# Routing per token tile, the norm vector folded into the router weights, and one expert of three groups moved to the conditional second round

## The chip, the cores and the metric

The kernel runs on one core of a Trainium2 chip. The metric is the time of one execution on the device, in microseconds (us), the median of three runs. TensorE (PE, with its weight loads listed as PEld), VectorE (DVE), ScalarE (ACT), GpSimd (POOL) and SyncE (SP) each work through a queue of their own; SP issues nearly all the weight loads. Lines (L107) are those of the kernel before, unless said otherwise.

## What is computed

Two transformer blocks on 256 tokens of width 1024, all in float32. The change is in the last part, a mixture of experts with two levels of routing. Cut to what matters:

```python
t = rmsnorm(h, norm_ffn)                                  # 256 x 1024
group_logits = t @ w_router_group                         # 8 groups
g_sel = argmax(group_logits);  p_group = softmax(group_logits)[g_sel]
in_group = (t @ w_router_expert).reshape(n, 8, 8)[rows, g_sel]
top_logit, top_local = top_k(in_group, 2)                 # 2 of the group's 8 experts
gate = softmax(top_logit) * p_group
hid = silu(x_e @ w_gate[e]) * (x_e @ w_up[e])             # 1024 -> 512, for each of 64 experts
y  += gate * (hid @ w_down[e])                            # 512 -> 1024
out = rmsnorm(h + y, norm_final)
```

The weights of one expert are three matrices of 2 MB each, so the 64 experts hold 403 MB, and most of the kernel's time goes into them.

## The kernel before

**Weights.** A float32 matrix is multiplied as two halves in a rounded type: `split` (L103 to L112) makes the high half `whi` on ACT (the hi cast) and the rest `wlo` on DVE (the lo, which reads whi), 128x1024 elements each, in buffers six deep. Each matmul of the program is then two or three on PE.

**Before the experts.** `out_proj` adds the output projection into the residual `xres`, for each of two token tiles t (128 tokens) and two column halves n. The four last pairs of weight rows are held back, so that the results come at the end one after another, (t, n) = (0,0), (0,1), (1,0), (1,1), and `router` is called for each. When both halves of a tile are there, it multiplies by the norm's gain `g_f2` into `tA`, transposes tA, multiplies by the router weights `wr` into the logits `lg` and scales by 1/rms. After both tiles a second piece of code picks each token's group (`G`, with `first_max`), its rank among the tokens of that group (`prk`, a matmul with a triangle of ones) and `key0`, the slot of tokens of group 0.

**The visits.** `moe` goes through groups of tokens in "visits": group 0, experts 0 to 2, first, because its weights can be loaded before the routing is known; then seven groups in order of size (place 1 is the smallest; which group that is, is known on the chip alone, in `which`), and group 0's experts 3 to 7 last. Place 7, the largest, has 128 slots and three products for each matmul ("large"); the others have 64 slots, where both halves of the tokens lie side by side and two products do. `prepare` makes the one-hot matrix `oh` of a visit, gathers its tokens by matmuls with tA (`pgx`), copies them (`xghi`, hi on ACT and lo on DVE) and gathers the gates of the visit's experts (`pgw`, from `wsel`). For each expert follow gate and up (`pgu`, 32 matmuls in a small visit), the activation, and down (`pd`). `plan` sorts the groups and makes their keys; `weights` makes wsel; `count` counts the tokens of each expert (`manyx`).

**Loads.** Weights go through a ring of 11 buffers of 1 MB, six loads for an expert (the last expert's down matrix in four halves of a load instead of two). SP issues them in order, each as soon as its buffer has been read. From the fourth expert on a load carries a condition: an expert with no tokens isn't loaded, but its buffers are passed over and all its arithmetic is done on what lies in them. The fourth expert's loads need `which` and `manyx`.

**The second round.** Tokens that find no slot in their group are counted by `beyond`; if there are any (`flag`), a second call of `moe` under a runtime condition takes two groups with 128 slots each, 16 experts.

**Order.** The order of instructions on each engine is set when the program is built, by a scheduler that goes by a cost model and by priorities (`with soon()` gives a high one), and by `fence`, which puts one instruction behind another. In the first visit the list `after` holds the fences of six splits: the first two have none, the next four stand behind the last copy of the router (`last_tT`). From step 8 of moe on (the end of the first expert's gate and up) PE, ACT and DVE keep the order of the program.

```python
on = after.pop() if after else None
for x in both:
    fence(x, on)
```

Of the kernel before, what the change touches and what calls it, by code (L numbers as in the profile page):

```python
# [32 lines left out]
def mega(ctx, tc, a, out, dbg=None):  # L33
# [978 lines left out]
    tAT = {}  # L1012

    rsq, last_tT = {}, [None]

    def router(t, n, ps):
        add_res(t, n, ps)
        if n == 0:
            rsq[t] = gp.tile([P, D], F32, tag="xn", name="xn"), sm.tile([P, 2], F32, tag="sh", name="sh")
        xn, ss = rsq[t]  # L1020
        nc.scalar.activation(xn[:, cols(n)], xres[:, t, cols(n)], AF.Square, accum_out=ss[:, n:n + 1])
        if n == 0:
            return
        if t == 0:
            tAT["A"] = mp.tile([P, NT, KD, P], F32, name="tA")
        tA = tAT["A"]
        tT = [mq.tile([P, 4, P], F32, tag="hid", name="tT") for _ in range(2)]
        by_k = lambda x: x.rearrange("q (p k) -> q k p", k=KD)
        for q in range(2):
            ks = slice(4 * q, 4 * q + 4)  # L1030
            nc.vector.tensor_tensor(tA[:, t, ks], by_k(xres[:, t, :])[:, ks], by_k(g_f2)[:, ks], op=OP.mult)
            ps = mm.tile([P, 4, P], F32, tag="mm", name="tps")
            for i in range(4):
                nc.tensor.transpose(ps[:, i, :], tA[:, t, 4 * q + i, :], ident)
            last_tT[0] = nc.scalar.copy(tT[q], ps)
        rs = inv_root(mean_sq(ss))
        ps = mm.tile([P, 512], F32, tag="mm", name="plg")
        for k in range(KD):
            nc.tensor.matmul(ps[:, :72], tT[k // 4][:, k % 4, :], wr[:, k, :], start=k == 0, stop=k == KD - 1)
        nc.vector.tensor_scalar(lg[:, t, :], ps[:, :72], rs, None, op0=OP.mult)  # L1040
        nc.vector.tensor_scalar(tA[:, t], tA[:, t], rs, None, op0=OP.mult)
# [3 lines left out]
    tA = tAT["A"]  # L1045
    dump("h1", xres)

    with soon():
        rdx = cst.tile([P, 8], F32, name="rdx")
        nc.gpsimd.iota(rdx, pattern=[[-1, 8]], base=8, channel_multiplier=0, allow_small_or_imprecise_dtypes=True)  # L1050
        slot = mp.tile([P, P], F32, name="slot")
        nc.gpsimd.iota(slot, pattern=[[1, P]], base=0, channel_multiplier=0, allow_small_or_imprecise_dtypes=True)
        slot2 = mp.tile([P, P], F32, name="slot2")
        nc.gpsimd.iota(slot2, pattern=[[0, 2], [1, GS]], base=0, channel_multiplier=0, allow_small_or_imprecise_dtypes=True)
        r1 = lambda n: mp.tile([P, NT], F32, name=n)
        r8 = lambda n: mp.tile([P, NT, 8], F32, name=n)

        def first_max(x, mx, oh):
            nt = x.shape[1]
            b8 = lambda x: x[:, :, None].to_broadcast([P, nt, 8])  # L1060
            nc.vector.tensor_reduce(mx, x, AX.X, OP.max)
            nc.vector.tensor_tensor(oh, x, b8(mx), op=OP.is_equal)
            nc.vector.tensor_tensor(oh, oh, rdx[:, None, :].to_broadcast([P, nt, 8]), op=OP.mult)
            m2 = sm.tile([P, nt], F32, tag="fm", name="fm")
            nc.vector.tensor_reduce(m2, oh, AX.X, OP.max)
# [510 lines left out]
```

## Time and profile before

| what | value |
|---|---|
| median of 3 runs | 1646.37 us (1645.75 to 1648.77) |
| profiled execution | 1646.35 us, its span 1644.6 us |
| PE busy | 1606.0 us, 98% of the span |
| DVE busy | 1353.3 us, 82% |
| ACT busy | 1148.5 us, 70% |
| DMA | 493.55 MB, 300 GB/s in the mean |

A matmul's end is modelled in such a profile, so that PE at 98% means that there is nearly always a matmul under way, not that the engine is at its peak. The shares are means over stages with different limits: the experts take the last 990 us, and it is there that the change is read.

### The profile page before, as it was taken

Reading aid. Unit: us, or ns where it says so; the run is one execution under the profiler, and the core shown is the slowest. Engines: PE = TensorE matmul, PEld = TensorE weight load, DVE = VectorE, ACT = ScalarE, POOL = GpSimd, SP = SyncE. Lnnn points to the kernel's source line nnn. Section 1 sums busy time; section 2 is a strip of 40 time slices with the busy share of each in tenths; the row PEclk is TensorE's granted clock in tenths of the full one; section 3 lists DMA queues with packets and bytes.
Section 4 is the critical chain, followed back from the end, with each engine's and each line's share of the span. In section 5 each row is a group of like instructions: output and inputs, shape, how many; then the busy total and the mean of one; then the engine's idle time right before and its main releaser. Section 6 shows DMA issues by size and latency. Waiting matters only on the chain. (4 is left out here: it accounts for less than half of the span.)

```text
span 1644.6 us, 24374 instructions
## 1 busy us (share of the span) xinstructions
PE 1606.0 (98%) x8474; PEld 1302.4 (79%) x8474; DVE 1353.3 (82%) x1643; ACT 1148.5 (70%) x1544; POOL 44.7 (3%) x69
## 2 busy tenths in 40 slices
PE   8999999999999998999999999999999999999996
PEld 7898788998798877777767777778877777777774
DVE  6666675555868886799999999998999899999997
ACT  5355554444556643788878888877788888888886
POOL 1000010000100130000000000000000000000000
PEclk9999999999999998999999999999999999999999
DMA  9953455555663337797997999999999999999991
GB/s 323 273 175 130 142 171 201 180 189 170 173 182 122 116 132 298 271 421 325 385 392 315 380 421 421 421 412 363 347 380 420 409 421 420 421 420 420 421 375 48
DMA packets 124884, 493.55 MB, mean 300 GB/s; under 512 B 9149, under 2 KB 53537, under 8 KB 78160
## 3 DMA queue, kind: packets, MB, share of 16 engines
q1 hardware_dynamic: 120160, 484.47, 76.9%
q0 software_dynamic: 1952, 6.05, 1.3%
q10 hardware_dynamic: 2640, 1.38, 0.3%
q8 instruction: 69, 1.13, 0.3%
q14 instruction: 63, 0.52, 0.1%
HBM read 509.30 MB, written 1.44 MB: 311 GB/s over the span
## 5 line engine op out<-in xcount | busy, mean ns | idle before, releaser
L107 DVE TENSOR_TENSOR wlo<-ring,whi 128x1024 fp32r<-128x1024 f32 x714 | 839.9, 1219 | 63.4 <-ACT whi L107 59.8
L107 ACT CAST whi<-ring 128x1024 fp32r<-128x1024 f32 x714 | 712.3, 1048 | 74.0 <-PE pgu L1279 20.9
L1279 PE MATMUL pgu<-whi,xghi 128*128 128x512 f32 x896 | 356.6, 398 | 1.4 <-DVE xghi L1216 1.4
L1280 PE MATMUL pgu<-wlo,xghi 128*128 128x512 f32 x896 | 352.8, 394 | 1.1 <-DVE wlo L107 1.1
L107 DVE TENSOR_TENSOR wlo<-raw,whi 128x1024 fp32r<-128x1024 f32 x173 | 211.8, 1232 | 135.6 <-ACT whi L107 134.3
L107 ACT CAST whi<-raw 128x1024 fp32r<-128x1024 f32 x173 | 180.3, 1048 | 188.9 <-PE pb L115 81.0
L1280 PEld LDWEIGHTS pgu<-wlo,xghi 128*128 128x128 f32 x896 | 169.4, 189 | 37.4 <-DVE wlo L107 3.4
L1279 PEld LDWEIGHTS pgu<-whi,xghi 128*128 128x128 f32 x896 | 169.4, 189 | 35.3 <-DVE xghi L1216 1.6
L114 PE MATMUL pb<-hThi,whi 128*128 128x256 f32 x480 | 137.5, 286 | 0.2 <-ACT hThi L129 0.2
L1279 PE MATMUL pd<-whi,hidThi 128*128 128x512 f32 x332 | 136.5, 411 | 0.9 <-DVE hidThi L1299 0.8
L115 PE MATMUL pb<-hTlo,whi 128*128 128x256 f32 x480 | 135.8, 283 | 0.5 <-DVE hTlo L130 0.5
L116 PE MATMUL pb<-hThi,wlo 128*128 128x256 f32 x480 | 135.7, 283 | 0.0
L1280 PE MATMUL pd<-wlo,hidThi 128*128 128x512 f32 x332 | 130.9, 394 | 0.0
L1289 PEld LDWEIGHTS pht<-pairs,gu 128*128 128x128 f32 x896 | 108.6, 191 | 4.9
L1289 PE MATMUL pht<-pairs,gu 128*128 128x64 f32 x896 | 106.0, 271 | 0.0
L1389 PE MATMUL pd<-ring,hs 128*64 128x512 f32 x216 | 104.2, 605 | 0.0
L1279 PEld LDWEIGHTS pd<-whi,hidThi 128*128 128x128 f32 x332 | 62.2, 187 | 52.8 <-ACT whi L107 36.1
L115 PEld LDWEIGHTS pb<-hTlo,whi 128*128 128x128 f32 x480 | 91.9, 191 | 1.4 <-DVE hTlo L130 0.7
L114 PEld LDWEIGHTS pb<-hThi,whi 128*128 128x128 f32 x480 | 91.9, 191 | 1.2 <-ACT hThi L129 0.5
L116 PEld LDWEIGHTS pb<-hThi,wlo 128*128 128x128 f32 x480 | 91.8, 191 | 0.0
L114 PE MATMUL pa<-whi,hThi 128*128 128x512 f32 x216 | 87.0, 406 | 3.3 <-ACT whi L107 1.7
L116 PE MATMUL pa<-whi,hTlo 128*128 128x512 f32 x216 | 85.6, 399 | 1.2 <-DVE hTlo L130 1.2
(432 smaller groups left out, 2260.1 us busy)
## 6 DMA issues: line engine op xcount, KB each, us to landing
ring<-in_w_gate_dram SPq DMA_DIRECT2D x128, 1024.0 KB, 9.9
ring<-in_w_up_dram SPq DMA_DIRECT2D x128, 1024.0 KB, 10.6
ring<-in_w_down_dram SPq DMA_DIRECT2D x126, 1024.0 KB, 9.2
raw<-in_w_in_dram SPq DMA_DIRECT2D x38, 1024.0 KB, 5.4
raw<-in_w_ff_dram SPq DMA_DIRECT2D x32, 1024.0 KB, 5.0
raw<-in_w_out_dram SPq DMA_DIRECT2D x12, 1024.0 KB, 5.0
raw<-in_w_in_dram SPq DMA_DIRECT2D x9, 512.0 KB, 4.8
raw<-in_w_ple_gate_dram SPq DMA_DIRECT2D x4, 1024.0 KB, 5.0
```

What stands on the lines that cost most here:

```text
L107: both = [nc.scalar.copy(hi, raw), nc.vector.tensor_tensor(lo, raw, hi.bitcast(F32), op=OP.subtract)]
L114: nc.tensor.matmul(ps, l[0][lsel], r[0][rsel], start=first, stop=False)
L115: nc.tensor.matmul(ps, l[0][lsel], r[1][rsel], start=False, stop=False)
L116: nc.tensor.matmul(ps, l[1][lsel], r[0][rsel], start=False, stop=last)
L1279: nc.tensor.matmul(ps, x[0][:, k, :], w[0][wsel], start=first, stop=False)
L1280: nc.tensor.matmul(ps, x[0][:, k, :], w[1][wsel], start=False, stop=last)
L1289: nc.tensor.matmul(ps[:, j, q, :], x[:, ts(q)], pairs, start=True, stop=True)
L1389: nc.tensor.matmul(pds[v][m][:GS, :], h[:, 3, :], wt[:, 0, cols(m)], start=False, stop=False)
```

## The change

Five parts. (1) The router's input is transposed straight from xres, each half as it is ready; the gain goes into the router weights once (`wr` times `gcol`, a new load of the gain by column), and three weight tensors get another order in memory on the host, so that rows fit. (2) Group, rank, key, one-hot and the gather of group 0 are done in `router`, for each token tile. (3) In `split` only the lo is fenced, and the fences of moe stand behind the last one-hot (`last_oh`). (4) `weights`, `plan` and `count` are called after steps 0, 3 and 4 of moe instead of ahead of it (the first two) and after step 0. (5) For group 0 (among experts 3 to 7) and places 1 and 2, `count` finds the expert with the fewest tokens, `trade` swaps it with expert 7 in the lists of names, counts and gates, and the last name of each list is left out of the visits. If any of the three has a token (`left`), the flag is set, and the second round then does these three as well as its 16.

```diff
-        for x in both:
-            fence(x, on)
+        fence(both[1], on)
...
+    gcol = mp.tile([P, KD], F32, name="gcol")
+    nc.gpsimd.dma_start(gcol, a["norm_ffn_2"].rearrange("(k p) -> p k", p=P))
+    nc.vector.tensor_tensor(wr, wr, gcol[:, :, None].to_broadcast([P, KD, NG + NG * NE]), op=OP.mult)
...
     def router(t, n, ps):
         add_res(t, n, ps)
...
+        tps = mm.tile([P, 4, P], F32, tag="mm", name="tps")
+        for i in range(4):
+            nc.tensor.transpose(tps[:, i, :], xres[:, t, (4 * n + i) * P:(4 * n + i + 1) * P], ident)
         nc.scalar.activation(xn[:, cols(n)], xres[:, t, cols(n)], AF.Square, accum_out=ss[:, n:n + 1])
+        tT = mq.tile([P, 4, P], F32, tag="hid", name="tT")
+        nc.scalar.copy(tT, tps)
+        for i in range(4):
+            nc.tensor.matmul(plg[t][:, :72], tT[:, i, :], wr[:, 4 * n + i, :], start=n + i == 0, stop=n + i == 4)
         if n == 0:
             return
+        rs = inv_root(mean_sq(ss))
+        nc.vector.tensor_scalar(lg[:, t, :], plg[t][:, :72], rs, None, op0=OP.mult)
+        tt_ = slice(t, t + 1)
+        first_max(lg[:, tt_, :8], gm[:, tt_], G[:, tt_])
+        ps = mm.tile([P, 512], F32, tag="mm", name="prk")
+        nc.tensor.matmul(ps[:, :8], ltm, G[:, t, :], start=True, stop=t == 0)
+        if t:
+            nc.tensor.matmul(ps[:, :8], ones, G[:, 0, :], start=False, stop=True)
+        nc.vector.scalar_tensor_tensor(tA[:, t].rearrange("p k f -> p (k f)"), xres[:, t, :], rs, g_f2, op0=OP.mult, op1=OP.mult)
...
+        last_oh[0] = nc.vector.tensor_scalar(oh0[:, t, :], slot2, key0[:, tt_], None, op0=OP.is_equal)
         if t == 0:
+            pgx0.append(acc.tile([P, KD, GS], F32, tag="acc", name="pgx"))
         for k in range(KD):
+            nc.tensor.matmul(pgx0[0][:, k, :], tA[:, t, k, :], oh0[:, t, :GS], start=t + k == 0, stop=t + k == KD)
...
-                nc.vector.tensor_scalar(ovi[:, 0:1], m, 0.0, None, op0=OP.is_gt)
+                nc.vector.tensor_tensor(ovi[:, 0:1], m, left, op=OP.max)
+                nc.vector.tensor_scalar(ovi[:, 0:1], ovi[:, 0:1], 0.0, None, op0=OP.is_gt)
...
+    def trade(x, at, n):
+        d, both = mp.tile([P, n, 8], F32, name="trd"), mp.tile([P, n], F32, name="trs")
+        nc.vector.tensor_tensor(d, x[:, :, 7:8].to_broadcast([P, n, 8]), x, op=OP.subtract)
+        nc.vector.tensor_tensor(d, d, at, op=OP.mult)
+        nc.vector.tensor_reduce(both, d, AX.X, OP.add)
+        nc.vector.tensor_tensor(x, x, d, op=OP.add)
+        nc.vector.tensor_tensor(x[:, :, 7], x[:, :, 7], both, op=OP.subtract)
...
+        nc.vector.scalar_tensor_tensor(few, many[:, :NS], 16.0, by3(rdx), op0=OP.mult, op1=OP.add)
+        nc.vector.memset(few[:, 0, :3], 1e6)
+        nc.vector.tensor_reduce(fewest, few, AX.X, OP.min)
+        nc.vector.tensor_tensor(few, few, fewest[:, :, None].to_broadcast([P, NS, 8]), op=OP.is_equal)
...
+        trade(many[:, :NS], few, NS)
+        trade(names, few, NS)
...
+        nc.vector.tensor_copy(namesx, names)
+        nc.vector.tensor_reduce(left, many[:, :NS, NE - 1], AX.X, OP.max)
...
+        nc.vector.tensor_copy(wsel2, wsel)
+        trade(wsel2, mine, NT)
...
-            for f in begin[:2]:
-                f()
-        after[:] = [last_tT[0]] * 4 + [None] * 2 if skip else []
+        after[:] = [last_oh[0]] * 4 + [None] * 2 if skip else []
...
                 if s == 0:
                     with soon():
+                        for f in begin[:1]:
+                            f()
                         finish([[0, prep]])
-                        for f in begin[2:]:
-                            f()
+                if 3 <= s < 2 + len(begin):
+                    begin[s - 2]()
...
     def in_order(g, e):
-        if g == 0:
-            return e
+        if g < NS:
+            return bass.ds(value(namesx[0:1, g, e:e + 1], NG * NE - 1), 1) if g or e > 2 else e
...
-        [(0, every[:3])] + [(g, every[3 * (g == 0):]) for g in (1, 2, 3, 7, 4, 5, 6, 0)],
-        small=lambda g: g < NG - 1, skip=True, begin=(plan, weights, count), on_the_way=beyond())
+        [(0, every[:3])] + [(g, every[3 * (g == 0):NE - (g < NS)]) for g in (1, 2, 3, 7, 4, 5, 6, 0)],
+        small=lambda g: g < NG - 1, skip=True, begin=(weights, plan, count), on_the_way=beyond())
...
     with tc.If(flag > 0):
+        for x in range(NS):
+            moe(lambda g: [(keys[:, t, g:g + 1] if g else key0[:, t:t + 1]) for t in range(NT)],
+                lambda g, e: bass.ds(lasts[g], 1), [(x, [NE - 1])], small=lambda g: True)
```

What the scheduler makes of it shows at three places. The first is the end of the output projection. On ACT, `xn,sh` are the squares of a half of xres (x3 and the last are those of all four halves), `tT` the copies of the transposed halves, and the `whi` are hi casts of the first experts' weights. Before:

```order
L1021 ACTIVATE xn,sh<-xres 128x512 x3
L1035 COPY tT<-tps 128x512
L1021 ACTIVATE xn,sh<-xres 128x512
L1035 COPY tT<-tps 128x512 x3
L107 CAST whi<-ring 128x1024 x4
```

and now:

```order
L1051 ACTIVATE xn,sh<-xres 128x512 x2
L1053 COPY tT<-tps 128x512
L107 CAST whi<-ring 128x1024
L1051 ACTIVATE xn,sh<-xres 128x512
L107 CAST whi<-ring 128x1024 x3
L1051 ACTIVATE xn,sh<-xres 128x512
L1053 COPY tT<-tps 128x512 x3
L1095 ACTIVATE tmp<-tmp 128x16
```

The four casts have moved from behind the router's copies to ahead of the last two squares. On DVE the same place now reads as follows (`xres<-xres,po` are the last two additions to the residual, `ms` the mean squares, `lg` the first tile's logits):

```order
L290 TENSOR_TENSOR xres<-xres,po 128x512
L272 TENSOR_SCALAR ms<-sh 128x1
L290 TENSOR_TENSOR xres<-xres,po 128x512
L273 SCALAR_TENSOR_TENSOR ms<-sh,ms 128x1
L1016 TENSOR_TENSOR wr<-wr,gcol 128x576
L1067 SCALAR_TENSOR_TENSOR tA<-xres,rs,g_f_5759 128x1024
L1059 TENSOR_SCALAR lg<-plg,rs 128x72
```

The product of wr and gcol, which every logit needs, stands behind the mean square of the second tile.

The second place is PE behind the output projection's last matmul (`po`): `plg` are the logits, `prk` the ranks, `pgx` the gather of group 0, `poh` a transpose of its one-hot. Before:

```order
L116 MATMUL po<-whi,hTlo 128x512
L1034 MATMUL tps<-ident,tA 128x128 x8
L1039 MATMUL plg<-wr,tT 128x72 x4
L1034 MATMUL tps<-ident,tA 128x128 x8
L1039 MATMUL plg<-wr,tT 128x72 x12
L1075 MATMUL prk<-G,ltm 128x8 x2
L1077 MATMUL prk<-G,ones 128x8
```

and now:

```order
L115 MATMUL po<-whi,hTlo 128x512
L1055 MATMUL plg<-wr,tT 128x72
L1050 MATMUL tps<-ident,xres 128x128 x4
L1055 MATMUL plg<-wr,tT 128x72 x7
L1064 MATMUL prk<-G,ltm 128x8
L1050 MATMUL tps<-ident,xres 128x128 x4
L1076 MATMUL pgx<-oh,tA 128x64 x3
L1290 MATMUL poh<-ident,oh 128x128
L1076 MATMUL pgx<-oh,tA 128x64 x5
L1055 MATMUL plg<-wr,tT 128x72
L1050 MATMUL tps<-ident,xres 128x128 x4
L1055 MATMUL plg<-wr,tT 128x72 x7
```

The logits of both tiles stood together, ahead of both ranks; now the rank and the gather of the first tile stand between them.

The third place is PE ahead of the second expert's gate, the `pgu` behind `pgw`; `pct<-sel` are the counts of each expert's tokens, `pgx` the gather of the next visit, and `wsel_6049` is the new wsel2. Before, the counts stood at the first expert's first matmul, and the second expert's gate began so:

```order
L1233 MATMUL pgx<-oh,tA 128x64 x13
L1245 MATMUL pgw<-wsel,oh 128x8 x2
L1248 MATMUL poh<-ident,oh 128x128 x2
L1279 MATMUL pgu<-whi,xghi 128x512
L1280 MATMUL pgu<-wlo,xghi 128x512
```

and now:

```order
L1322 MATMUL pgu<-wlo,xghi 128x512
L1217 MATMUL pct<-sel,ones 128x64 x2
L1276 MATMUL pgx<-oh,tA 128x64 x8
L1290 MATMUL poh<-ident,oh 128x128
L1276 MATMUL pgx<-oh,tA 128x64 x8
L1290 MATMUL poh<-ident,oh 128x128
L1287 MATMUL pgw<-wsel_6049,oh 128x8 x2
L1321 MATMUL pgu<-whi,xghi 128x512
```

The counts, the whole gather and the gates from wsel2, the last product of `count`, now stand between the first expert's up and the second expert's gate.

## Rows read from the trace of the kernel before

**Rows 1.** Windows: PE, PEld, DVE, ACT, POOL busy (instructions), granted clock, DMA share, GB/s.

```profile
1300.00:1400.00 100.00, 100.00 (x480) 76.03 (x479) 94.46 (x99) 85.19 (x107) 0.00 (x0) 1.00 1.01 421
```

**Rows 2.** Waits from 700 to 1600 us: in total, times, longest.

```profile
ACT whi L107 <- DMA ring<-in_w_down_dram: 0.7, 2, 0.3
```

**Rows 3.** SP's timeline in place 2: the down loads of three experts in turn.

```profile
911.28 0.66 SPq L99 DMA_DIRECT2D ring<-in_w_down_dram  x2
...
925.22 1.16 SPq L99 DMA_DIRECT2D ring<-in_w_down_dram  x2
...
939.15 1.14 SPq L99 DMA_DIRECT2D ring<-in_w_down_dram  x2
```

**Rows 4.** DMA moved and issued from 652 to 1638 us, with median us to landing.

```profile
q1 hardware_dynamic: 50976, 369.12, 92.4%
...
ring<-in_w_down_dram SPq DMA_DIRECT2D x124, 1024.0 KB, 9.2
ring<-in_w_gate_dram SPq DMA_DIRECT2D x122, 1024.0 KB, 9.4
ring<-in_w_up_dram SPq DMA_DIRECT2D x122, 1024.0 KB, 10.7
```

**Rows 5.** The view of rows 1 in two stretches of 14 us.

```profile
766.00:780.00 14.00, 14.00 (x84) 11.34 (x84) 11.23 (x14) 10.22 (x14) 0.00 (x0) 1.00 0.38 138
884.00:898.00 14.00, 14.00 (x76) 11.06 (x75) 13.14 (x15) 10.83 (x14) 0.00 (x0) 1.00 0.34 132
```

**Rows 6.** The DMA view of rows 4, from 1545 to 1570 us.

```profile
ring<-in_w_down_dram SPq DMA_DIRECT2D x4, 1024.0 KB, 17.4
```

**Rows 7.** PE's timeline: start, duration, and idle time ahead with its releaser.

```profile
633.84 0.39 PE L116 MATMUL po<-whi,hTlo 128*128 128x512 f32 x1
...
646.54 0.57 PE L1075 MATMUL prk<-G,ltm 128*128 128x8 f32 x2 [5.64 <-DVE G L1066]
...
652.00 3.51 PE L1233 MATMUL pgx<-oh,tA 128*128 128x64 f32 x16
656.92 0.80 PE L1279 MATMUL pgu<-whi,xghi 128*128 128x512 f32 x1 [1.40 <-DVE xghi L1216]
...
672.71 0.48 PE L1279 MATMUL pgu<-whi,xghi 128*128 128x512 f32 x1
```

**Rows 8.** ACT's timeline: the square of the last half of xres.

```profile
635.24 0.63 ACT L1021 ACTIVATE xn<-xres 128x512 f32<-128x512 f32 x1
```

**Rows 9.** The page's groups of instructions: the two halves of a split, mean ns.

```profile
L107 DVE TENSOR_TENSOR wlo<-ring,whi 128x1024 fp32r<-128x1024 f32 x714 | 839.9, 1219 | 63.4 <-ACT whi L107 59.8
L107 ACT CAST whi<-ring 128x1024 fp32r<-128x1024 f32 x714 | 712.3, 1048 | 74.0 <-PE pgu L1279 20.9
```

**Rows 10.** DVE's timeline in the routing and the plan.

```profile
639.18 0.28 DVE L1040 TENSOR_SCALAR lg<-plg,rs 128x72 f32<-128x72 f32 x1
...
640.29 0.17 DVE L1066 TENSOR_TENSOR G<-G,fm 128x8 f32<-128x8 f32 x1
...
646.23 0.17 DVE L1066 TENSOR_TENSOR G<-G,fm 128x8 f32<-128x8 f32 x1
...
648.21 0.28 DVE L1225 TENSOR_SCALAR oh<-slot,key 128x128 f32<-128x128 f32 x1
...
651.94 0.17 DVE L1129 SCALAR_TENSOR_TENSOR size<-pct,rdx 128x8 f32<-128x8 f32 x1 [1.23 <-PE pct L1123]
...
655.41 0.18 DVE L1152 TENSOR_TENSOR keys<-keys,rank 128x16 f32<-128x16 f32 x1
...
658.41 0.17 DVE L1251 COPY gw<-pgw 128x8 f32<-128x8 f32 x1 [1.54 <-PE pgw L1245]
658.49 0.47 DVE L1225 TENSOR_SCALAR oh<-slot,keys 128x128 f32<-128x128 f32 x2
```

**Rows 11.** The view of rows 1 during the first expert's gate.

```profile
657.00:664.00 7.00, 7.00 (x21) 5.84 (x22) 2.91 (x6) 2.32 (x3) 0.00 (x0) 0.50 0.01 2
```

**Rows 12.** DMA issues from 560 to 650 us: the router weights' smaller load.

```profile
wr<-in_w_router_group_dram POOLq DMA_DIRECT2D x1, 32.0 KB, 6.6
```

More of the change, by code (lines that the diff above doesn't have):

```diff
@@ L1043, in mega @@
     for _ in wo2:
         pass
-    tA = tAT["A"]
     dump("h1", xres)
[L1048 to L1065, printed above, removed]
-            nc.vector.tensor_tensor(oh, oh, b8(m2), op=OP.is_equal)
-        gm, G, tmp, rank, key0 = r1("gm"), r8("G"), r8("tmp"), r1("rank"), r1("key0")
-        ranked = []
-        for t in range(NT):
-            tt_ = slice(t, t + 1)
-            first_max(lg[:, tt_, :8], gm[:, tt_], G[:, tt_])
-            ps = mm.tile([P, 512], F32, tag="mm", name="prk")
-            nc.tensor.matmul(ps[:, :8], ltm, G[:, t, :], start=True, stop=t == 0)
-            if t:
-                ranked.append(nc.tensor.matmul(ps[:, :8], ones, G[:, 0, :], start=False, stop=True))
-            nc.vector.tensor_scalar(key0[:, tt_], G[:, t, 0:1], -4096.0, 4096.0, op0=OP.mult, op1=OP.add)
-            nc.vector.tensor_tensor(tmp[:, t, :], ps[:, :8], G[:, t, :], op=OP.mult)
-            nc.vector.tensor_reduce(rank[:, tt_], tmp[:, t, :], AX.X, OP.add)
-            nc.vector.tensor_tensor(key0[:, tt_], key0[:, tt_], rank[:, tt_], op=OP.add)
@@ L1118, in weights @@
         dump("wsel", wsel)
+    at_ = mp.tile([P, 8], F32, name="at_")
     def plan():
@@ L1192, in beyond @@
         beyonds["flag"] = nc.values_load(ovx[0:1, 0:1], min_val=0, max_val=1, skip_runtime_bounds_check_because="it is 0 or 1")
+    NS = 3
+    namesx = mp.tile([P, NS, 8], I32, name="namesx")
+    left = mp.tile([P, 1], F32, name="left")
+    wsel2 = r8("wsel2")
+    def trade(x, at, n):
[5 more added lines that the diff above has]
+        nc.vector.tensor_tensor(x[:, :, 7], x[:, :, 7], both, op=OP.subtract)
     def count():
@@ L1219, in two, with prepare @@
         return x.rearrange("p k (a b) -> p k a b", a=2)
-    def prepare(keys, b, small, xgs, gws, v):
-        oh = mq.tile([P, NT, P], F32, name="oh", bufs=1)
-        for t in range(NT):
-            nc.vector.tensor_scalar(oh[:, t, :], slot2 if small else slot, keys[t], None, op0=OP.is_equal)
-        yield
+    def prepare(keys, b, small, xgs, gws, v, wsel):
         xg = [x[:, b] for x in xgb]
@@ L1229, in prepare @@
         kn = 512 // w
-        pss = [acc.tile([P, kn, w], F32, tag="acc", name="pgx") for _ in range(KD // kn)]
-        for t in range(NT):
+        oh, pss = oh0, pgx0[:]
+        if not pss:
+            oh = mq.tile([P, NT, P], F32, name="oh", bufs=1)
+            for t in range(NT):
+                nc.vector.tensor_scalar(oh[:, t, :], slot2 if small else slot, keys[t], None, op0=OP.is_equal)
+            yield
+            pss = [acc.tile([P, kn, w], F32, tag="acc", name="pgx") for _ in range(KD // kn)]
+        for t in range(0 if pgx0 else NT):
             for k in range(KD):
-                x = nc.tensor.matmul(pss[k // kn][:, k % kn, :], tA[:, t, k, :], oh[:, t, :w],
+                nc.tensor.matmul(pss[k // kn][:, k % kn, :], tA[:, t, k, :], oh[:, t, :w],
                                      start=t == 0 and k % kn == 0, stop=t == 1 and k % kn == kn - 1)
-                if t + k == 0 and ranked:
-                    fence(x, ranked.pop())
         yield AHEAD
@@ L1240, in prepare @@
             halves(two(xg[0]), ps) if small else split_ps(xg[0][:, ks, :], xg[1][:, ks, :], ps)
+        pgx0.clear()
         xgs[v] = xg
@@ L1337, in mega, with moe @@
     AHEAD = 3
-    def moe(keys, expert, visits, small=lambda g: False, skip=False, begin=(), on_the_way=iter(())):
+    weights_ = wsel
+    def moe(keys, expert, visits, small=lambda g: False, skip=False, begin=(), on_the_way=iter(()), wsel=wsel2):
+        first = weights_ if skip else wsel
         todo = [(v, g, e, es) for v, (g, es) in enumerate(visits) for e in es]
@@ L1426, in follow @@
                     g2 = visits[v + 1][0]
-                    steps.append([1, prepare(keys(g2), (v + 1) % 2, small(g2), xgs, gws, v + 1)])
+                    steps.append([1, prepare(keys(g2), (v + 1) % 2, small(g2), xgs, gws, v + 1, wsel)])
                 if i == 0 and kind == "u" and last:
```

72 lines of the change are left out of this document (47 added, 25 removed).

## Prediction

> **What bounds the kernel now.** I read the windows by stage first. In a stretch of small visits PE is busy all the time, DVE 94%, and DMA runs at 421 GB/s [rows 1]: three limits close together, so the question is which ends last. The waits decide it: over nearly the whole expert stage ACT waits 0.7 us in all for a down load to land [rows 2], so the loads come in time and the chain of hi cast, lo and matmul sets the pace. That pace is the distance from one expert's loads to the next on SP, which follows the reading of the buffers: 13.94 and 13.93 us [rows 3]. DMA is right behind: six loads of 1.049 MB at 421 GB/s are 14.94 us, more than 13.93, and only the extra work where a visit ends lets the loads keep up.
>
> **Do the three experts fall away at all?** The change rests on three experts without a token, one in each of group 0's late list and places 1 and 2; otherwise the flag is set. From 652 to 1638 us SP issued 124, 122 and 122 loads of 1.0486 MB, and the last expert's four halves, 387.97 MB, but 369.12 MB moved [rows 4]. The 18.85 MB that are missing are 18 loads, which is three experts. Two holes in the DMA stand at 766 and 884 us, 138 and 132 GB/s [rows 5]; a third must be hidden in the backlog near the end. They are 118 us apart, eight experts of 13.93 and 6.6 for what a visit adds, so they have the same place in two visits that follow each other. The reference's inputs, worked through in float32, give the same: expert 6 of groups 0, 6 and 5 has no token, and those are group 0 and the two smallest. No group overflows. So the lists lose just these three and the flag stays 0.
>
> **Term 1, three experts less.** Their loads were skipped already; what goes is their arithmetic, which has no condition. A buffer's turn is 11 loads of 13.93/6 us, 25.5 us, so the expert that left the hole at 884 us is worked off from about 910 us; there SP's rows keep the same pace [rows 3], and an empty expert costs as much as another. 3 x 13.93 = 41.8 us. The cover for this saving is the ring: without the holes the loads must keep up for 25 experts from the start to the large visit. From 1545 to 1570 us, after 24 small experts since the large one, a load lands 17.4 us after its issue [rows 6], of the 25.5 of a turn. So 24 experts used up all but 8 us, and 25 should just pass; the large visit then refills the lead. I take 41.8 and keep a loss of up to 8 us for a rival.
>
> **Term 2, the first expert's start.** Before, the last matmul of the output projection starts at 633.84 and the first expert's at 656.92 [rows 7], 23.1 us later. The order now, from that last matmul (L, 0.5 us later than before because four transposes stand in front of it):
> The unfenced hi casts stand ahead of the last square on ACT. Each needs a buffer that the held-back rows release only with their last matmuls, and takes 1.05 us [rows 9]; three in a row from there put the square at about L+3.3, where it was 1.4 behind [rows 8, 7].
> Behind it DVE has the mean square, the wr product (an estimate of 0.7 from the lo's 1.22 by elements [rows 9]) and only then PE the first tile's logits: 24 short instructions of 0.11 us. (The gather's sixteen took 3.51 us at half clock, 0.22 each [rows 7]; I use 0.11 at full clock.) Logits at L+8.
> The first tile's choice of group took 1.28 us (639.18 to 640.46 [rows 10]); with rank, key and one-hot 2.8: L+10.8.
> PE then has the first gather ahead of the second tile's logits: 18 instructions, four transposes, a copy of 0.6, the last logits: 4.2 us at full clock, 7.5 at half. Second logits at L+15 to 18.3.
> Its choice is again 1.28, and from G to the end of the one-hot 2.1 (646.40 to 648.49 [rows 10]): L+18.4 to 21.7.
> DVE then has four fenced lo's, 4.9 us, and four small operations ahead of the lo of the gathered tokens, 0.7, while gather and copy take 2.6 to 4.5: first expert at L+24.7 to 28.0, against 23.1. With L's 0.5 that is +2.1 to +5.4; if the casts don't hold the square, +0.2. I take +4. So the earlier selection buys nothing here: what was parallel over two tiles is now one tile after the other, and the scheduler has put the whole of it behind the output projection.
> The new load gcol is in pieces of 4 bytes, as many as the 32 KB router load has, which landed in 6.6 us [rows 12]; it is issued right behind the router loads, which were there for the first logits before, and its product stands late by its place on DVE, so it costs nothing. If it comes later than that product's turn, term 2 grows by the rest.
>
> **Term 3, the second expert's start.** Before, the second expert's gate began at 672.71, 15.8 us after the first one's [rows 7], because plan and count were done by then. Now, from the first expert's start F:
> The group counts on PE stand behind sixteen gate matmuls. At half clock, as granted from 657 to 664 [rows 11], a 512-column matmul starts each 0.43 us (512 columns at 1.2 GHz): F+7.4, size at F+8.
> From size to the last key took 3.65 us (651.94 to 655.59), the two one-hots 0.47 [rows 10]; five lo's of 1.22 now lie between: F+18.2 for the one-hots, F+17.5 for the selection (sel) that the counts need.
> PE has run out at F+11.5 (sixteen more matmuls at full clock) and waits some 6 us for that selection; then come counts and 36 short instructions of the gather, to F+22.4 at full clock, F+26.3 at half.
> On DVE some 28 small operations follow, of count and trade, at 0.18 each (3.65 over 20) 5.1 us: wsel2 at F+23.2 (F+21.2 at 0.11).
> The gates from wsel2 need 0.3 to 0.8 more; then the second expert's gate: F+22.7 to F+27.1, and if the clock is at half, its sixteen matmuls take 3.3 us longer. Against 15.8: +6.9 to +14.6. A wait on PE of this kind, 5.64 us ahead of prk [rows 7], was followed by half clock for the gather and the gate [rows 7, 11], so I lean to the upper half: +11.5.
> All this holds only if a matmul that waits holds up those behind it. DVE shows the like: the one-hots, whose keys were done at 655.59, started at 658.49, behind a copy that had waited 1.54 us for PE [rows 10]. The Trainium skill (TensorE: Matmul & The Clock Gate, Step-by-step: what each phase is for) says that matmuls stay in program order and only weight loads are pulled ahead. By that rule the pgw that waits for wsel2 keeps back matmuls whose weights are ready; without it term 3 would be near 0 and the kernel 37.8 us faster.
> SP waits as well: the fourth expert's loads now need namesx, at about F+22.5, and wait for it. Sixteen loads are there by then, enough for the second and third expert, so this costs nothing of its own.
>
> The fences also change the first 20 us, where two hi casts move ahead of the first copies of hT: 1 us either way, taken as 0. Loads in the new memory order have the same pieces.
>
> **Sum.** Against the profiled execution, 1646.35 (span 1644.6; the median, 1646.37, is the same): -41.8 + 4 + 11.5 = -26.3, or 1620.0 us. With the bounds: -41.8 + 0.2 + 6.9 = -34.7 and -41.8 + 5.4 + 14.6 = -21.8; with 1 us for the start, 1611 to 1626.
>
> **Rivals.** (A) The routing gains what it seems written for: the first tile's part runs beside the second's output projection. The second tile alone would then need (from L) square 1.4, logits 2, choice and one-hot 3.4, gather, copy and lo 3.3 to 5: some 12 us instead of 23.1, and the plan's operations fall on a DVE that has time. -41.8 - 11 + 0 to 8: 1594 to 1602. For it: the gap is there, and DVE idles in it. Against it: the rows of the order, where wr and the first logits come last.
> (B) DMA becomes the bound, as only skipped loads gave it room: up to 8 us lost before the large visit, 1621 to 1632. For it: 17.4 of 25.5 us. Against it: the extra work at each visit's end, which refills.
> (C) Slower: a token on one of the three experts sets the flag, and the second round runs. It decides at a single token, and costs the three experts again and 16 large ones with three products each, 48 and 24 matmuls of 512 columns at 2.4 GHz, 0.213 us, 15.4 us: 1620 + 42 + 16 x 15.4, 1908 us at least. Against it are the 18 missing loads.
> (D) The swap saves nothing because skipped experts were cheap: 1646 + 15.5, 1662 us. The even pace over an empty expert [rows 3] speaks against it.
>
> **Chances.** Forecast 0.68; A 0.13; B 0.13; C 0.03; D 0.03. The time forecast is 1620; the range 1602 to 1632 takes in B, the edge of A and errors of a few us in a chain of some forty steps. A change within 0.2% (3.3 us) can hardly be told from none. Faster 0.93, same 0.02, slower 0.05.
>
> **What would show it.** Right: 53 small experts on PE instead of 56 (848 pgu matmuls of each half instead of 896), no hole in the DMA at 770 and 890 us, the same 13.93 between experts, a first expert's matmul near 661 us, PE idle 5 to 7 us behind the first expert's up, and the second gate near 687 us. Wrong: a first matmul before 650 us (A), waits of hi casts for loads in places 2 and 3 (B), a branch into the second round (C), or PE going on past the counts.

## The result, and the profile after

The changed kernel takes 1630.1 us (median of 4 runs, 1626.1 to 1631.5) against 1647.0 for the kernel before (4 runs, 1645.8 to 1648.8): a ratio of 0.9893 (95% interval 0.9872 to 0.9914). It was forecast faster by 26.3 us and is faster by 16.8. The profiled execution took 1629.16 us with a span of 1627.5, 17.1 less than before. Lines from here on are those of the kernel that a row is from.

The page's groups of instructions, after the change: the small experts' gate and up on PE.

```profile
L1321 PE MATMUL pgu<-whi,xghi 128*128 128x512 f32 x848 | 339.1, 400 | 2.2 <-DVE xghi L1257 1.7
L1322 PE MATMUL pgu<-wlo,xghi 128*128 128x512 f32 x848 | 334.2, 394 | 1.0 <-DVE wlo L107 1.0
```

Each half has 848 matmuls, as said, so 53 small experts are worked through. SP's timeline after, beside [rows 3]:

```profile
911.90 1.10 SPq L99 DMA_DIRECT2D ring<-in_w_down_dram  x2
925.78 1.06 SPq L99 DMA_DIRECT2D ring<-in_w_down_dram  x2
939.66 1.14 SPq L99 DMA_DIRECT2D ring<-in_w_down_dram  x2
```

An expert still takes 13.88 us. The waits from 700 to 1600 us, to be held against [rows 2]:

```profile
PEld pd L1434 <- DMA ring<-in_w_down_dram: 1.8, 5, 0.4
ACT whi L107 <- DMA ring<-in_w_up_dram: 0.9, 3, 0.3
ACT whi L107 <- DMA ring<-in_w_down_dram: 0.6, 2, 0.3
```

Transfers hold PE and ACT up by 3.3 us in these rows, of 900. All rows of this kind add up to 4.0 us, against 6.2 in the kernel before (there [rows 2] and five more), so rival B did not happen. It came closer, though: from 1545 to 1570 us a load now takes 17.8 to 19.7 us in the median from issue to landing, of the 25.5 of a turn (17.4 in [rows 6]):

```profile
ring<-in_w_down_dram SPq DMA_DIRECT2D x4, 1024.0 KB, 17.8
ring<-in_w_gate_dram SPq DMA_DIRECT2D x4, 1024.0 KB, 19.7
```

So the experts went as forecast. The loss is in front of them. PE's timeline after, for [rows 7]; the first row is the last matmul of the first block's output projection.

```profile
226.97 0.40 PE L115 MATMUL po<-whi,hTlo 128*128 128x512 f32 x1
...
231.13 0.50 PE L113 MATMUL ppj<-whi,pThi 128*128 128x512 f32 x1 [1.49 <-DVE prj L580]
...
237.61 0.38 PE L113 MATMUL pb<-hThi,whi 128*128 128x256 f32 x1 [1.15 <-ACT hThi L128]
240.29 0.58 PE L114 MATMUL pb<-hTlo,whi 128*128 128x256 f32 x1 [2.29 <-DVE hTlo L129]
...
642.71 0.39 PE L115 MATMUL po<-whi,hTlo 128*128 128x512 f32 x1
...
647.24 0.68 PE L1055 MATMUL plg<-wr,tT 128*128 128x72 f32 x2 [4.14 <-ACT xn L1051]
...
671.60 0.79 PE L1321 MATMUL pgu<-whi,xghi 128*128 128x512 f32 x1 [1.66 <-DVE xghi L1257]
...
687.72 1.08 PE L1217 MATMUL pct<-sel,ones 128*128 128x64 f32 x4 [4.87 <-DVE sel L1213]
...
696.46 0.77 PE L1321 MATMUL pgu<-whi,xghi 128*128 128x512 f32 x1
...
717.02 0.47 PE L1321 MATMUL pgu<-whi,xghi 128*128 128x512 f32 x1
```

In the kernel before the first of these places read:

```profile
225.51 0.40 PE L116 MATMUL po<-whi,hTlo 128*128 128x512 f32 x1
...
233.47 0.38 PE L114 MATMUL pb<-hThi,whi 128*128 128x256 f32 x1 [0.24 <-ACT hThi L129]
234.35 0.38 PE L115 MATMUL pb<-hTlo,whi 128*128 128x256 f32 x1 [0.50 <-DVE hTlo L130]
```

(PE waits for no `prj` there.) 642.71 is 8.9 us later than before, of which the forecast had priced 0.5, for four transposes. ACT's timeline after shows what stands there, at the first block's feed-forward part (225 to 240 us) and at the end of the second output projection:

```profile
225.41 2.00 ACT L107 CAST whi<-raw 128x1024 fp32r<-128x1024 f32 x2 [1.93 <-issue]
...
234.98 1.05 ACT L107 CAST whi<-raw 128x1024 fp32r<-128x1024 f32 x1 [3.49 <-issue]
...
236.04 1.03 ACT L107 CAST whi<-raw 128x1024 fp32r<-128x1024 f32 x1
236.98 1.07 ACT L128 CAST hThi<-tps 128x512 fp32r<-128x512 f32 x2
...
642.69 2.92 ACT L107 CAST whi<-ring 128x1024 fp32r<-128x1024 f32 x3
645.52 0.62 ACT L1051 ACTIVATE xn<-xres 128x512 f32<-128x512 f32 x1
```

The two copies `hThi`, which the feed-forward matmuls `pb` read, stand behind a cast that began at 234.98, after 3.49 us of idle time for which the row names no releaser. DVE works off two lo's (228.1 to 230.5) ahead of the copy `prj`, and four (234.4 to 239.6) ahead of `hTlo`. The windows, with the columns of [rows 1], tell what PE's waits were followed by:

```profile
240.00:246.00 6.00, 5.71 (x26) 5.71 (x27) 2.03 (x4) 0.57 (x1) 0.00 (x0) 0.50 0.94 300
...
646.00:676.00 30.00, 23.09 (x94) 21.15 (x95) 15.85 (x58) 5.43 (x11) 1.05 (x1) 0.50 0.33 129
686.00:706.00 20.00, 18.28 (x73) 16.96 (x74) 8.90 (x46) 5.67 (x8) 0.00 (x0) 0.51 0.28 105
766.00:780.00 14.00, 14.00 (x66) 10.52 (x66) 13.76 (x14) 12.92 (x16) 0.00 (x0) 1.00 1.02 421
884.00:898.00 14.00, 14.00 (x74) 10.93 (x73) 13.66 (x16) 11.10 (x14) 0.00 (x0) 1.00 0.97 406
```

The granted clock was 0.50 (0.51 in the third row), the lower level of 1.2 GHz, behind each of the three waits, in the middle one for 30 us. (At these places the kernel before has 0.50 only once, for 20 us, 644 to 664; [rows 11] are a part of it.) The holes of [rows 5] are filled.

**One table for all kernels.** Five stretches between points on PE's timeline (us): to the last matmul of the first output projection (S), from there to the last of the second (A), to the first expert's gate (B), to the third expert's gate (C), and to the end of the span (D). The medians are of all runs, the stretches of the profiled one. Each ratio is to the kernel before as measured beside that kernel, where its median was 1646.5 to 1648.8.

| kernel | median | ratio, 95% | S | A | B | C | D |
|---|---|---|---|---|---|---|---|
| before (64 experts) | 1647.0 | 1 | 225.5 | 408.3 | 23.1 | 31.8 | 955.9 |
| after (61) | 1630.1 | 0.9893, 0.9872 to 0.9914 | 227.0 | 415.7 | 28.9 | 45.4 | 910.5 |
| e1 (61) | 1619.9 | 0.9835, 0.9820 to 0.9849 | 228.2 | 408.7 | 28.0 | 42.7 | 910.5 |
| e2 (64) | 1655.7 | 1.0054, 1.0041 to 1.0066 | 226.8 | 414.9 | 25.5 | 30.7 | 955.9 |
| e3 (64) | 1668.5 | 1.0137, 1.0119 to 1.0155 | 226.8 | 415.4 | 28.9 | 42.6 | 951.7 |
| e4 (61) | 1625.7 | 0.9863, 0.9847 to 0.9879 | 227.6 | 416.5 | 25.7 | 44.9 | 910.4 |
| e5 (61) | 1615.2 | 0.9810, 0.9796 to 0.9823 | 225.5 | 407.7 | 28.9 | 40.6 | 910.6 |
| e6 (61) | 1605.7 | 0.9754, 0.9741 to 0.9768 | 225.6 | 408.3 | 23.1 | 31.9 | 914.8 |
| e7 (61) | 1622.5 | 0.9853, 0.9838 to 0.9869 | 225.4 | 408.8 | 28.7 | 45.2 | 910.7 |
| e8 (61) | 1615.2 | 0.9809, 0.9796 to 0.9823 | 226.5 | 407.8 | 28.7 | 40.6 | 910.4 |
| e9 (61) | 1603.5 | 0.9747, 0.9734 to 0.9761 | 225.6 | 409.2 | 21.2 | 30.9 | 915.0 |
| e10 (61) | 1614.9 | 0.9806, 0.9792 to 0.9819 | 225.8 | 408.8 | 30.0 | 38.0 | 910.7 |
| e11 (61) | 1621.4 | 0.9851, 0.9836 to 0.9866 | 225.6 | 407.8 | 30.1 | 44.2 | 911.0 |

From before to after: S +1.5, A +7.4, B +5.8, C +13.7, D -45.4, together the -17.1 of the span (rounded terms). S varies by up to 2.8 us whatever the fences are, so nothing of it is laid to the change: e1 has the fences of before and the longest S, and ran from 205.5 to 208.9 us of it at a granted clock of 0.50. C has such a spread too, within one order of instructions: the second expert, from its gate to the third's, took 20.6 us in the changed kernel and 17.7 and 17.6 in e1 and e3. In e3 the clock rose some 7 us earlier, where the changed kernel's row above has 0.51:

```profile
686.00:706.00 20.00, 18.75 (x87) 17.43 (x88) 10.21 (x45) 7.53 (x11) 0.00 (x0) 0.66 0.34 119
```

So a difference of up to 3 us in C between two single profiles says nothing by itself.

### The profile page after: what moved, and what is told of

Same layout as the page of the kernel before. It is cut to its first block, busy times and chain, and to the rows that moved or that the text cites. A ratio compares the mean times of both kernels' runs of the same rounds, so it can differ in the third digit from the quotient of the medians.

```text
span 1627.5 us, 23716 instructions
## 1 busy us (share of the span) xinstructions
PE 1575.8 (97%) x8282; PEld 1284.1 (79%) x8282; DVE 1315.1 (81%) x1631; ACT 1112.5 (68%) x1499; POOL 47.8 (3%) x70
## 5 line engine op out<-in xcount | busy, mean ns | idle before, releaser
L107 DVE TENSOR_TENSOR wlo<-ring,whi 128x1024 fp32r<-128x1024 f32 x681 | 801.1, 1220 | 62.1 <-ACT whi L107 58.8
L107 ACT CAST whi<-ring 128x1024 fp32r<-128x1024 f32 x681 | 680.4, 1049 | 70.7 <-PE pgu L1321 20.7
L1321 PE MATMUL pgu<-whi,xghi 128*128 128x512 f32 x848 | 339.1, 400 | 2.2 <-DVE xghi L1257 1.7
L1322 PE MATMUL pgu<-wlo,xghi 128*128 128x512 f32 x848 | 334.2, 394 | 1.0 <-DVE wlo L107 1.0
L1322 PEld LDWEIGHTS pgu<-wlo,xghi 128*128 128x128 f32 x848 | 161.3, 190 | 34.9 <-DVE wlo L107 2.7
L1321 PEld LDWEIGHTS pgu<-whi,xghi 128*128 128x128 f32 x848 | 161.5, 190 | 34.4 <-DVE xghi L1257 1.8
L1321 PE MATMUL pd<-whi,hidThi 128*128 128x512 f32 x314 | 128.1, 408 | 1.3 <-DVE hidThi L1341 1.3
L1322 PE MATMUL pd<-wlo,hidThi 128*128 128x512 f32 x314 | 123.1, 392 | 0.0
L1331 PEld LDWEIGHTS pht<-pairs,gu 128*128 128x128 f32 x848 | 104.5, 194 | 4.9
L1434 PE MATMUL pd<-ring,hs 128*64 128x512 f32 x204 | 98.5, 605 | 0.0
```

The source lines that it names most:

```text
L1321: nc.tensor.matmul(ps, x[0][:, k, :], w[0][wsel], start=first, stop=False)
L1322: nc.tensor.matmul(ps, x[0][:, k, :], w[1][wsel], start=False, stop=last)
L1331: nc.tensor.matmul(ps[:, j, q, :], x[:, ts(q)], pairs, start=True, stop=True)
L1434: nc.tensor.matmul(pds[v][m][:GS, :], h[:, 3, :], wt[:, 0, cols(m)], start=False, stop=False)
```

## The experiments

**e1 and e2: the fence of the hi half, put back and taken away alone.** e1 is the changed kernel with

```diff
-        fence(both[1], on)
+        for x in both[1 if ring else 0:]:
+            fence(x, on)
```

(`ring` is empty until the expert part), and e2 the kernel before with only the change's own `fence(both[1], on)`.

> The changed kernel, with the order fence on both halves again everywhere before the expert part (hi casts there go behind the named copy or square as before the change); in the expert part only lo stays fenced. Theory F: the 8.4 us by which everything from 250 to 634 us is late come from unfenced hi casts that stand ahead of hT's copies and of the squares on ScalarE, 1.5 at the start and 6.9 at the first feed-forward block. Then the time falls by 8.4, from 1630 to about 1621.5, and the wait on hTlo near 240 us (2.29 us) and the half clock behind it are gone. Rival M: the lateness comes from the loads (their order in memory, other transfers), and the time stays at 1629 to 1631.

> The kernel before, with one edit: only the lo half of a split weight is fenced, as in the changed kernel. Theory F: 8.4 us are lost before the expert part, and some 2 to 4 more at its start, where three hi casts of 1.05 us stand ahead of the last square: 1655 to 1659. Rival M: nothing changes before the expert part: 1647 to 1650.

Both times are near what theory F has, and stretch A shows it. e1's PE timeline:

```profile
236.13 0.38 PE L114 MATMUL pb<-hThi,whi 128*128 128x256 f32 x1 [0.24 <-ACT hThi L129]
237.02 0.38 PE L115 MATMUL pb<-hTlo,whi 128*128 128x256 f32 x1 [0.50 <-DVE hTlo L130]
...
636.91 0.39 PE L116 MATMUL po<-whi,hTlo 128*128 128x512 f32 x1
...
664.93 0.79 PE L1322 MATMUL pgu<-whi,xghi 128*128 128x512 f32 x1 [1.65 <-DVE xghi L1258]
```

In e1, A is 408.7 as in the kernel before, and the granted clock from 240 to 246 us is 1.00; in e2 A is 414.9, near the changed one. The starts of the same matmuls tell it closer. Held against the kernel before, the changed one is 1.5 us late at 226 us and 8.4 late from 241 us on, e2 1.2 and 8.2, e1 2.7 at both. So the fence is worth 6.9 to 7.0 us, all of it at that place. The part of theory F on the start is refuted: S was longest in e1. That e1's span is 9.3 us below the changed kernel's, and not 7.0, is 2.8 of C and 0.9 of B, with S 1.2 the other way; the 2.8 are within the spread of C. e2 also prices the casts ahead of the last square with the old routing: B grew by 2.4 us, while C fell by about 1.

**e3: the three experts visited again.**

```diff
-        [(0, every[:3])] + [(g, every[3 * (g == 0):NE - (g < NS)]) for g in (1, 2, 3, 7, 4, 5, 6, 0)],
+        [(0, every[:3])] + [(g, every[3 * (g == 0):]) for g in (1, 2, 3, 7, 4, 5, 6, 0)],
```

> The changed kernel with the three least used experts visited again at the end of their group's list (64 experts in the visits, the trade still worked out, the output the same). If an expert without tokens costs as much as another, 3 x 13.93 us come back: 1630 + 41.8, about 1672, and up to 3 us more where the pace differs. Rival D, empty experts are cheap since their loads are skipped: under 1640.

The time is 38.3 us over that of the changed kernel, 3.5 short of the 41.8 that were expected. D is 41.2 longer, 13.7 for each expert; the rest is stretch C, 2.8 shorter here with the same calls (the clock, as told above). Rival D falls: an expert without tokens costs what another does.

**e4: the product of router weights and gain, earlier.**

```diff
-        add_res(t, n, ps)
+        x = add_res(t, n, ps)
+        if t and n == 0:
+            fence(x, wr_gain)
```

(`add_res` hands back its instruction, and `wr_gain` is the product.)

> The changed kernel with one more order fence: the product of router weights and gain goes ahead of the residual addition of the second tile's first half on VectorE, instead of behind the last mean square; gcol landed at 629.5 us, the product then stands near 640. Theory W: TensorE's wait of 4.1 us ahead of the first logits is this product's place; the first expert starts 4 us earlier, or up to 8 if the clock stays up: 1622 to 1626. Rival S: the second tile's square, root and logits set the start anyway, and the time stays within 1 us of 1630.

B is 25.7 instead of 28.9, and the median is in the range of theory W. But the edit did more than was meant: the second tile's first half, now behind the product, was overtaken by its second half, whose addition waits for the last matmul of the output projection (L at 644.04). DVE's timeline:

```profile
644.47 0.69 DVE L290 TENSOR_TENSOR xres<-xres,po 128x512 f32<-128x512 f32 x1 [2.33 <-PE po L115]
645.08 0.75 DVE L1016 TENSOR_TENSOR wr<-wr,gcol 128x576 f32<-128x576 f32 x1
```

So the product came 1.0 us behind L, not near 640. The intervals of the two ratios overlap; it is B that carries this.

**e5 and e10: plan, weights and count called earlier**, both on top of e1. e5 calls all three behind step 0, e10 as the kernel before does: plan and weights ahead of the first expert's matmuls, count behind step 0. e10's edit:

```diff
             while 0 not in xgs:
                 next(prep)
+            for f in (begin[1], begin[0]) if begin else ():
+                f()
...
-                        for f in begin[:1]:
-                            f()
                         finish([[0, prep]])
-                if 3 <= s < 2 + len(begin):
-                    begin[s - 2]()
+                        for f in begin[2:]:
+                            f()
```

> The kernel of e1 (hi casts fenced before the expert part), and plan, weights and count called behind step 0 as before the change, not behind steps 0, 3 and 4. Measured against e1's 1619.9. Theory Q: TensorE's 4.9 us of waiting for sel behind the first expert's up, and the half clock behind it, come from the late call: plan's small operations stand behind five lo's. Called early, the second expert's gate comes 16 to 19 us behind the first one's instead of 25, and the second expert runs at full clock: 9 to 13 us less, 1607 to 1611. Rival R: the small operations now delay the first expert's own lo's by as much: 1618 to 1621.

> The changed kernel with hi casts fenced before the expert part (as e1 and e5), and plan and weights called ahead of the first expert's matmuls, count behind step 0: the calls of the kernel before with the new routing. e5 (all three behind step 0) gained 4.8 of the 9 to 13 that were expected, since the second gate still waited 2.98 us for wsel2. If the late place of plan and weights is what is left, the second gate comes 16 to 17 us behind the first one's (20.5 in e5, 25.0 in e1) and the time is 1609 to 1612, provided that the first expert starts no later. If the small operations now delay the first expert instead, it stays at 1614 to 1617.

Both medians are about half as far below e1's as theory Q says, and e10's lies in the range of its second alternative. But S and A, which come before all these calls, make 3.7 of e5's 4.8 us in the profiles, and 2.4 of e10's 5.0; B and C together are 1.2 and 2.7 shorter. Up to the second gate the early calls do gain: it comes 20.5 and 18.5 us behind the first one, 25.0 in e1, though not the 16 to 19 (e5) and 16 to 17 (e10) that were expected. The second expert then takes 20.1 and 19.5 us, 17.7 in e1, so that C falls only from 42.7 to 40.6 and 38.0; B grew to 28.9 and 30.0. e5's PE timeline shows the wait going on to the next product:

```profile
662.11 0.80 PE L1322 MATMUL pgu<-whi,xghi 128*128 128x512 f32 x1 [1.55 <-DVE xghi L1258]
...
681.74 1.00 PE L1288 MATMUL pgw<-wsel,oh 128*128 128x8 f32 x4 [2.98 <-DVE wsel L1209]
682.59 0.77 PE L1322 MATMUL pgu<-whi,xghi 128*128 128x512 f32 x1
```

The wait for sel is 1.00 us there (4.86 in e1), and 2.98 for wsel2 come in its place. The late call explains a part of C only.

**e6: the trade alone, on the kernel before.** All of `trade`, `count`, the visits and the second round from the change; the routing, the fences, the memory order and the order of calls from before.

```diff
-        if g == 0:
-            return e
+        if g < NS:
+            return bass.ds(value(namesx[0:1, g, e:e + 1], NG * NE - 1), 1) if g or e > 2 else e
...
-        [(0, every[:3])] + [(g, every[3 * (g == 0):]) for g in (1, 2, 3, 7, 4, 5, 6, 0)],
+        [(0, every[:3])] + [(g, every[3 * (g == 0):NE - (g < NS)]) for g in (1, 2, 3, 7, 4, 5, 6, 0)],
```

> The kernel before, with only the trade and the conditional second round added: routing, fences, memory order and the order of plan, weights and count as before. If three experts are worth 41 us by themselves and the trade's some 28 small operations cost 0 to 5: 1604 to 1611, faster than the whole change. If the trade's chain delays the second expert by itself, as it does in the changed kernel: 1612 to 1620. If the saving needs the new routing: over 1625.

It takes 1605.7 us, 24.4 less than the whole change. Its PE timeline:

```profile
633.94 0.39 PE L116 MATMUL po<-whi,hTlo 128*128 128x512 f32 x1
...
657.01 0.79 PE L1318 MATMUL pgu<-whi,xghi 128*128 128x512 f32 x1 [1.40 <-DVE xghi L1255]
...
673.00 0.48 PE L1318 MATMUL pgu<-whi,xghi 128*128 128x512 f32 x1
...
688.95 0.47 PE L1318 MATMUL pgu<-whi,xghi 128*128 128x512 f32 x1
```

The second gate comes 16.0 us behind the first, as in [rows 7] (15.8), though all the operations of the trade stand on DVE. The DVE timeline tells why: `sel` is made ahead of the first expert in this kernel, and 15.8 us behind its first matmul in the changed one. First e6, then the changed kernel:

```profile
655.02 0.36 DVE L1213 TENSOR_TENSOR sel<-keys__6020,osel 128x64 f32<-128x64 f32 x2
...
659.44 0.22 DVE L1219 COPY many<-pct 128x64 f32<-128x64 f32 x1 [0.39 <-PE pct L1217]
```

```profile
687.36 0.35 DVE L1213 TENSOR_TENSOR sel<-keys__6039,osel 128x64 f32<-128x64 f32 x2
...
688.84 0.23 DVE L1221 COPY many<-pct 128x64 f32<-128x64 f32 x1 [0.53 <-PE pct L1217]
```

**e7, e8 and e11: the casts and the last square.** e7 is meant to put the expert part's hi casts behind the last square, with the head's fences of e1 and e4's early product; e8 adds e5's calls; e11 fences both halves everywhere, which puts the casts behind the one-hot.

```diff
+        fence(both[0], last_sq[0] if ring and on else on)
         fence(both[1], on)
...
```

(`last_sq` is the latest square that `router` has made; e4's lines, and for e8 those of e5, are left out here.)

> The changed kernel with hi casts fenced before the expert part, the expert part's hi casts fenced behind the last square, and the product of router weights and gain ahead of the second tile's residual addition as in e4. Measured against e1's 1619.9. By the prediction's second term the three casts hold the last square for about 2 us, and e4 gained 3 to 4 by the product: 1613 to 1617. Rival: casts that go behind the square delay the first expert's weights instead, and only the product's gain is left or less: 1617 to 1621.

> e7 with plan, weights and count behind step 0 as in e5. If the three losses (head, first expert, second expert) are separate, their gains add: 1600 to 1607. If TensorE's half clock joins them, so that only the longest wait counts, it is no better than the best of e5 and e7 by over 2 us.

> The changed kernel with both halves fenced everywhere, the expert part too: its hi casts go behind the one-hot. Against e1 this tells what the hi casts cost that stand ahead of the last square: by the prediction's second term about 2 us, so the first gate 26 us behind the last output projection matmul instead of 28.0, and 1617 to 1618.5. Rival: the casts, now late, delay the first expert's own weights: 1620 to 1623.

e7 missed, over both of its ranges, and didn't do what it was for. Its two edits clash: as in e4 the halves of the second tile change places, so the casts do stand behind the square of the second half (635.31), but the first half's square is now the last, behind all four of them. Its ACT timeline:

```profile
635.93 3.87 ACT L107 CAST whi<-ring 128x1024 fp32r<-128x1024 f32 x4
639.71 0.62 ACT L1054 ACTIVATE xn<-xres 128x512 f32<-128x512 f32 x1
```

That square starts 5.6 us behind the last matmul (2.8 in the changed kernel), so e7 says nothing on what the casts cost. e8 gives 1615.2, like e5. That is the number of its second alternative, but with e7's part not doing its work it doesn't tell whether the losses are separate. In e11 the squares are free, the last at 634.47, 1.2 behind the last matmul; but DVE has tA's product ahead of the router weights' now:

```profile
636.06 1.28 DVE L1068 SCALAR_TENSOR_TENSOR tA<-xres,rs,g_f 128x1024 f32<-128x1024 f32 x1 [0.68 <-POOL rs L279]
637.26 0.75 DVE L1017 TENSOR_TENSOR wr<-wr,gcol 128x576 f32<-128x576 f32 x1
```

The product ends 4.7 us behind the last matmul instead of 4.4, and PE waits 2.58 us for the first expert's `xghi`, behind the late lo's, instead of 1.66. B is 30.1, and the time is in the rival's range. So putting the casts behind the one-hot gains nothing here; what they cost where they stood was not told apart from the new order on DVE.

**e9: e6 with the new memory order.**

```diff
-        by_k = lambda x: x.rearrange("q (p k) -> q k p", k=KD)
+        by_k = lambda x: x.rearrange("q (k p) -> q k p", k=KD)
...
-        if name == "w_down_2":
+        if name in ("w_gate_2", "w_up_2", "w_down_2", "w_router_group_2", "w_router_expert_2"):
```

(The host reorders each of these in blocks of 128 rows.)

> The kernel of e6 (the kernel before with the trade alone), with one more part of the change: gate, up and router weights are laid out in memory as in the changed kernel, and tA's halves are read from xres in plain order. From the third expert's gate to the end e6 takes 4.3 us more than the changed kernel (914.8 against 910.5) over the same experts. If the memory order, or what it moves in on-chip memory, is what makes the rest faster, this one takes about 910.5 there and 1601 in all; if not, it takes 914 to 915 there and 1604 to 1607 in all.

D stays at 915.0, so the memory order is not what makes the changed kernel's D 4.3 us shorter. But B is 21.2 and C 30.9, each about the shortest of all (e2's C is 30.7); why was not shown. 1603.5 us is the lowest median here, 26.6 below the whole change; its interval overlaps e6's.

## Why the prediction was right, and where it was off

- **The sign, and term 1 (-41.8): right.** Three experts are worth 41.2 us in D by e3 (951.7 against 910.5) and 41.1 by e6 (955.9 against 914.8). The loads kept up, and no second round ran: it would have added 288 us to D by rival C's price.
- **The step that failed** is "The fences also change the first 20 us, where two hi casts move ahead of the first copies of hT: 1 us either way, taken as 0." It prices one place only. The fence list is filled again for the first block's feed-forward part, 200 us on (`after[:] = [last_copy[0]] * 4 + [sqs[1, 1]] * 2`). There the unfenced casts cost 6.9 to 7.0 us of A (e1, e2): waits of 1.49, 1.15 and 2.29 us (none, 0.24 and 0.50 before), and half clock from 240 to 246 us.
- **Where the 9.2 us between forecast (-26.3) and span (-17.1) went.** These 7 us in A, S 1.5, term 2 2.3 and term 3 2.2 are against the forecast; 3.6 of D, which nobody forecast, are for it (rounded terms). The forecast's own range, 1611 to 1626, missed by 4 us. That the wide one held is luck in part: it was drawn for rival B, the edge of A and small errors, not for a loss in the first block, and D gave some of that back.
- **Term 2 (+4): under-sized.** From L on it says +3.5, and B measures +5.8. The last square started near where forecast, at L+2.8 (estimate L+3.3). But PE was at half clock from 646 us on, where full clock was used for the first tile's logits: the first expert came at L+28.9, just over the upper bound of 28.0. (gcol landed 9.0 us after its issue, not 6.6, at 629.5; its product stood at 646.38, so this cost nothing, as said.)
- **Term 3 (+11.5): right in kind and nearly in size.** The second gate came at F+24.9 (said: F+22.7 to 27.1), PE idled 4.87 us behind the first expert's up (said: some 6), the cause being sel behind the lo's. To that come 4.6 us in the second expert at half clock, where 3.3 had been bounded (1.7 in e1 and e3, where the clock rose earlier): C grew by 13.7, inside the 14.6 of the upper bound. PE idled for `pct` until 687.72 though the six splits that come next, the second expert's whole gate among them, were done at 686.1. This agrees with what the prediction takes from the Trainium skill (TensorE: Matmul & The Clock Gate, Step-by-step: what each phase is for), that matmuls stay in program order. It was not `pgw` that waited, as the prediction has it: wsel2 was done at 692.3, and PE came to `pgw` at 695.75. In e5 and e10, with the earlier calls, `pgw` did wait.
- **Not forecast: D is 3.8 to 4.6 us shorter** wherever the new routing is in (910.4 to 911.0, with e6 and e9 at 914.8 and 915.0; 951.7 against 955.9 for 64 experts). The order of instructions on PE, ACT and DVE is the same there in e6 and in the changed kernel, and e9 rules the memory order out. The gain comes evenly, some 0.06 us in a small expert, and the starts of PE's matmuls show where: up to 1600 us the down matmuls with whi and wlo (372 each in e6) follow one another at 242.8 and 240.3 ns in the mean, at 246.1 and 244.1 in e6, and those of gate and up (944 each) are 0.6 to 0.7 ns closer, which makes some 2.6 and 1.2 of the 4 us. Why they follow closer stays open.
- **The rivals.** A (the routing gains) is refuted: the new routing with its fences and calls costs 19.3 us more than the old in B and C, and 13.0 with the old calls (e10 against e6). B's range holds the time, but its mechanism did not occur; C and D did not either.

e10 has the old calls and the new routing, and C is still 6.1 us longer than in e6. Its trace tells the parts apart: up to the second gate it is 2.5 longer, about the wait for wsel2 (2.43 us), and 3.6 in the second expert, which ran at half clock until 691 us:

```profile
683.00:691.00 8.00, 8.00 (x28) 7.03 (x29) 1.55 (x3) 3.76 (x4) 0.00 (x0) 0.50 0.70 262
```

## What to carry to other kernels

When a helper changes what it orders, go through every place that calls it, and not only the part that the change is about: the 7 us were lost 400 us ahead of it, and the order of ACT's instructions there had changed for all to see. Work cut out of the engine that is busy all the time was worth its full length here (41 us for three experts), also where its transfers were skipped already. Small operations that move from a gap that an engine has anyway (old routing: DVE idle while PE gathers) into a stretch where it is full can cost more than their durations: here PE waited 4.87 us for them and came back at half clock, and calling them earlier gained 4.5 to 6.5 us up to the second gate. And where the clock decides, a few us of one profile can be chance; compare the same stretch in several kernels that share its instructions.

## What the runs showed of the hardware that was not expected

- In the changed kernel the granted clock stayed at 0.50, the level of 1.2 GHz, for 30 us (646 to 676) though PE was busy 23.09 of them: with transposes and matmuls of 64 and 72 columns, waits of 1.0 to 1.7 us between them, and from 671.6 on the first expert's matmuls of 512 columns without a gap, during which it rose.
- Behind the same wait (4.87 us in the changed kernel) and the same instructions it then stayed at 0.50 until about 707 us there; e3 has a granted clock of 0.96 from 699 to 706 us, where the changed kernel has 0.50.
- The first output projection ended between 225.4 and 228.2 us in kernels that have the same fences there (e7 and e1); e1 alone has a stretch of granted clock 0.50 in front of it, with PE busy throughout (205.5 to 208.9 us).
